# Large on-chip tiles moved to multiples of 512 bytes in a two-layer hybrid backbone

## The chip, the cores and the metric

The kernel runs on one core of a Trainium2 chip. The metric is the device time of one execution in microseconds (us), the median of several runs.

## What is computed

Two layers (DEPTH = 2) over 256 latent tokens and 256 context tokens of width 1024, all in float32. Each layer is a SwiGLU feed-forward block, a token mixer and a second SwiGLU block; each of the three takes its input through a shift and a scale, and its output goes through a gate, is added to the scaled residual and normalised. Shift, scale and gate come from a conditioning vector by a wide matrix, `w_ada`.

```
def ffn_sublayer(xs, m, j, wg, wu, wd, g, b):
    y = MACARON * swiglu(modulate(xs, m, j), wg, wu, wd)
    return residual_post_norm(xs, m[3 * j + 2] * y, g, b)
...
for l in range(DEPTH):
    m_lat = (jax.nn.silu(c) @ w_ada[l] + b_ada[l])...
    x_lat = ffn_sublayer(x_lat, m_lat, 0, ff1_gate[l], ff1_up[l], ff1_down[l], ...)
    x_ctx = ffn_sublayer(x_ctx, m_ctx, 0, ff1_gate[l], ff1_up[l], ff1_down[l], ...)
    y_lat, y_ctx = hybrid_mixer(modulate(x_lat, m_lat, 1), modulate(x_ctx, m_ctx, 1), ...)
    x_lat = residual_post_norm(x_lat, m_lat[5] * y_lat, ...)
    x_lat = ffn_sublayer(x_lat, m_lat, 2, ff2_gate[l], ff2_up[l], ff2_down[l], ...)
```

The mixer has neighbourhood attention (8 heads), a bidirectional gated recurrence and a Fourier branch, between one input and one output projection. The feed-forward width is 2816.

## The kernel before, in words

Activations are held transposed: 128 partitions are 128 of the 1024 channels, `xT[:, j, :]` is channel block j of 8, and its 512 columns are the 256 context and the 256 latent tokens. The large products are made at near float32 accuracy from three float32r matmuls: activations are split into a rounded part and a remainder (`hH`, `hL` for the input of a block, `aH`, `aL` for its middle), weights into `whi` and `wlo`, and hi x hi, hi x lo and lo x hi are summed (`mmh`, line 391). Each matmul has weights of 128x128 and streams 256 columns. Their results are named `gu` (gate and up), `dn` (down), `head` and `pj` (input projection of the mixer) and `wo` (output projection). `sc` are the attention scores, made from the tiles `k` and `q`.

Weights come in pieces of 128x1024 float32 (512 KB, `raw`, five buffers, issued on SP's queue at lines 254 and 256), ScalarE rounds a piece to `whi` (line 274), and VectorE, or for some pieces GpSimd, subtracts to get `wlo` (line 591). Rows of `w_ada` come through the same five buffers and are multiplied into `acc` and `fold` tiles by VectorE (lines 298 to 304). The first 15 us load x and the context into `in` tiles (line 237) and the constants into `cs`, and TensorE transposes x to `xT`.

The order of the whole program is fixed in the code (lists `seq` and `ORDER`). The on-chip memory is laid out by the order in which the pools are opened and, in the pool `const`, by the order in which the tiles are asked for; each tile begins at the next multiple of 32 bytes of a partition. A partition's row of a `raw`, `whi`, `wlo` or `acc` tile is 4096 bytes, of the tiles in the pool `scr` (tag "s", 13 buffers, with `k`, `sg`, `pr`, `h32` and others) 2048 bytes.

Of the kernel before, what the change touches and what calls it, by code (L numbers as in the profile page):

```python
# [11 lines left out]
F32 = mybir.dt.float32  # L12
# [7 lines left out]
DEPTH = 2  # L20
D = 1024
KD = D // 128
# [43 lines left out]
def kernel(ctx: ExitStack, tc: tile.TileContext, x, cx, vecs, cst, bias, w_ada,  # L66
# [3 lines left out]
    const = ctx.enter_context(tc.tile_pool(name="const", bufs=1))  # L70
# [10 lines left out]

    V, S, G, PE = nc.vector, nc.scalar, nc.gpsimd, nc.tensor

    xT = const.tile([128, KD, 512], F32, name="xT")
    hH = const.tile([128, KD, 512], F32R, name="hH")
    hL = const.tile([128, KD, 512], F32R, name="hL")
# [7 lines left out]
    SN = cs[:, 896:1408].rearrange("p (a b) -> p a b", a=2)  # L94
    vT = const.tile([128, V_ROWS], F32, name="vT")
    onesD = const.tile([128, 128], F32, name="onesD")
    one_c = const.tile([128, 1], F32, name="one_c")
    pick = const.tile([128, 2, 2], F32, name="pick")
    scol = const.tile([128, KD, 2], F32, name="scol")
    join = const.tile([128, 2], F32, name="join")  # L100
    bmean = const.tile([128, 6], F32, name="bmean")
    kcol = const.tile([128, 8], F32, name="kcol")
    lbd = const.tile([128, 8, 128], F32, name="lbd")
    fbd = const.tile([128, 2, 128], F32, name="fbd")
    AB = const.tile([128, 2, 2, 128], F32, name="AB")
    scol_z = AB[:, 0].rearrange("p a (k s) -> p (a k) s", s=32)
    mcol = [const.tile([128, 2, 72], F32, name=f"mcol{l}") for l in range(DEPTH)]

    def vcol(name, i, n=1):
        o = V_OFF[name] + i  # L110
# [1300 lines left out]
```

## Time and profile before

| | us |
|---|---|
| median of 3 runs (lowest, highest) | 1830.83 (1827.59, 1833.77) |
| the profiled execution | 1830.9 |
| its span, first to last instruction | 1829.0 |
| TensorE busy | 1751.4 |
| VectorE busy | 1224.8 |
| ScalarE busy | 700.6 |
| GpSimd busy | 327.9 |

The mean granted TensorE clock over the span is 0.983. Busy times overlap one another, so they do not add up to the span; 1.9 us of the execution lie outside it.

### The profile page before, as it was taken

The numbers are of one execution on the slowest core, as the hardware profiler recorded it, in microseconds if no ns is written. First come the engines' busy times: TensorE is split into PE (matmuls) and PEld (weight loads), VectorE is DVE, ScalarE is ACT, GpSimd is POOL, SyncE is SP. The second block draws the span as 40 slices with busy tenths as digits, with TensorE's granted clock in tenths as the row PEclk, the third lists the DMA queues.
The fourth block names the chain that finished last, engine by engine and source line by source line (L and its number), as shares of the span: only waits on it lengthen the run. The fifth ranks groups of instructions, "written<-read, shape, count | busy, mean of one in ns | idle before, by whom it ended". The sixth has DMA issues, their size and how long they took to land.

```text
span 1829.0 us, 33865 instructions
## 1 busy us (share of the span) xinstructions
PE 1751.4 (96%) x14241; PEld 1698.2 (93%) x14241; DVE 1224.8 (67%) x1867; ACT 700.6 (38%) x1119; POOL 327.9 (18%) x258
## 2 busy tenths in 40 slices
PE   7999999999899999999999999999999988979997
PEld 5999999998788999999999999999999868869997
DVE  3799899837586488755664569844643759666555
ACT  2232222225756564312222363222222565555443
POOL 0142122215441061000000140000000545140000
PEclk9999999999999999999999999999999999989998
DMA  7566555532223226544453226555653233266662
GB/s 263 181 195 187 170 167 170 171 95 81 69 59 93 59 82 180 162 139 136 132 157 114 86 81 196 166 171 166 178 169 88 81 93 93 82 192 192 177 190 80
DMA packets 375080, 253.33 MB, mean 139 GB/s; under 512 B 8144, under 2 KB 336336, under 8 KB 374928
## 3 DMA queue, kind: packets, MB, share of 16 engines
q1 hardware_dynamic: 373856, 248.81, 46.3%
q8 instruction: 112, 1.84, 0.4%
q0 software_dynamic: 1072, 2.36, 0.4%
q14 instruction: 40, 0.33, 0.1%
HBM read 250.09 MB, written 1.05 MB: 137 GB/s over the span
## 4 chain that ended last, share of the span: by engine, by line
PE 79%; DVE 15%; ACT 3%; issue 2%; DMA 0%; POOL 0%; SPq 0%; DVEq 0%; ACTq 0%
PE gu L391 42%; PE dn L391 21%; PE head L391 5%; PE pj L391 3%; PE wo L391 2%; DVE acc L304 2%; PE adat L332 1%; DVE ri L903 1%; DVE wlo L591 1%; PE o L1097 1%; DVE xl L870 1%; DVE s L460 1%; DVE xT L718 1%; DVE s L463 1%; PE adap L315 1%
## 5 line engine op out<-in xcount | busy, mean ns | idle before, releaser
L391 PE MATMUL gu<-hH,whi 128*128 128x256 f32 x2336 | 500.1, 283 | 2.0 <-ACT hH L1262 1.8
L391 PE MATMUL gu<-hH,wlo 128*128 128x256 f32 x2336 | 497.4, 282 | 2.1 <-DVE wlo L591 2.1
L391 PE MATMUL gu<-hL,whi 128*128 128x256 f32 x2336 | 497.6, 282 | 1.2 <-DVE hL L591 1.1
L274 ACT CAST whi<-raw 128x1024 fp32r<-128x1024 f32 (+1 forms) x319 | 318.8, 1024 | 284.3 <-PE dn L391 104.8
L591 POOL TENSOR_TENSOR wlo<-raw,whi 128x1024 fp32r<-128x1024 f32 (+2 forms) x106 | 207.7, 1966 | 1191.3 <-ACT whi L274 1153.7
L391 PEld LDWEIGHTS gu<-hH,whi 128*128 128x128 f32 x2336 | 374.1, 190 | 5.9 <-ACT hH L1262 2.6
L391 PEld LDWEIGHTS gu<-hH,wlo 128*128 128x128 f32 x2336 | 373.9, 190 | 2.6 <-DVE wlo L591 2.6
L391 PEld LDWEIGHTS gu<-hL,whi 128*128 128x128 f32 x2336 | 374.1, 190 | 1.7 <-DVE hL L591 1.7
L591 DVE TENSOR_TENSOR wlo<-raw,whi 128x1024 fp32r<-128x1024 f32 (+1 forms) x245 | 295.5, 1209 | 92.8 <-ACT whi L274 89.5
L391 PE MATMUL dn<-aH,whi 128*128 128x256 f32 x1280 | 286.3, 283 | 0.8 <-DVE xT L718 0.8
L391 PE MATMUL dn<-aH,wlo 128*128 128x256 f32 x1280 | 283.6, 281 | 0.0
L391 PE MATMUL dn<-aL,whi 128*128 128x256 f32 x1280 | 283.6, 281 | 0.0
L304 DVE SCALAR_TENSOR_TENSOR acc<-raw,scol,acc 128x512 f32<-128x512 f32 x337 | 275.2, 864 | 1.0
L731 ACT CAST aH<-pr 128x512 fp32r<-128x512 f32 (+1 forms) x88 | 50.0, 568 | 422.9 <-DVE pr L730 422.9
L391 PEld LDWEIGHTS dn<-aH,whi 128*128 128x128 f32 x1280 | 208.7, 189 | 1.4 <-DVE xT L718 1.2
L391 PEld LDWEIGHTS dn<-aH,wlo 128*128 128x128 f32 x1280 | 208.7, 189 | 0.1
L391 PEld LDWEIGHTS dn<-aL,whi 128*128 128x128 f32 x1280 | 208.7, 189 | 0.0
L730 DVE TENSOR_TENSOR pr<-sg,gu 128x512 f32<-128x512 f32 (+1 forms) x84 | 51.5, 614 | 148.7 <-PE gu L391 146.2
L718 DVE SCALAR_TENSOR_TENSOR xT<-dn,gate,xT 128x256 f32<-128x256 f32 x174 | 78.0, 478 | 90.5 <-PE dn L391 90.0
L729 ACT ACTIVATE sg<-gu 128x512 f32<-128x512 f32 (+1 forms) x84 | 45.3, 539 | 115.5 <-PE gu L391 115.3
L391 PE MATMUL pj<-hH,whi 128*128 128x256 f32 x384 | 84.5, 288 | 4.9 <-DVE k L591 2.7
L391 PE MATMUL pj<-hH,wlo 128*128 128x256 f32 x384 | 83.1, 285 | 0.0
(239 smaller groups left out, 2127.7 us busy)
## 6 DMA issues: line engine op xcount, KB each, us to landing
raw<-in_w_ada_dram SPq DMA_DIRECT2D x136, 512.0 KB, 4.6
raw<-in_ff_gate_dram SPq DMA_DIRECT2D x88, 512.0 KB, 4.4
raw<-in_ff_up_dram SPq DMA_DIRECT2D x88, 512.0 KB, 4.8
raw<-in_ff_down_dram SPq DMA_DIRECT2D x64, 448.0 KB, 4.5
raw<-in_w_in_dram SPq DMA_DIRECT2D x36, 512.0 KB, 3.9
raw<-in_ff_down_dram SPq DMA_DIRECT2D x32, 512.0 KB, 4.8
raw<-in_w_out_dram SPq DMA_DIRECT2D x16, 512.0 KB, 4.1
in<-in_w_ada_dram SPq DMA_DIRECT2D x8, 512.0 KB, 6.9
```

Of the source, the lines that this page charges most:

```text
L274: S.copy(h_[:, :n], t[:, :n])
L304: V.scalar_tensor_tensor(out=a[:, st], in0=t[:, kk * 512:(kk + 1) * 512], scalar=sc_, in1=a[:, st], op0=ALU.mult, op1=ALU.add)
L315: PE.matmul(acc[l, b][32 * (k % 4):32 * (k % 4) + 32, :], lhsT=scol_z[:, k, :], rhs=t[:, kk * 512:(kk + 1) * 512], start=(k < 4), stop=(k ...
L332: PE.matmul(tp[:, q * 2:q * 2 + 2], lhsT=a[:, q * 128:(q + 1) * 128], rhs=w, start=True, stop=True)
L391: PE.matmul(o[:, c], lhsT=w, rhs=X[:, k, c], start=first and i == 0, stop=last and i == len(halves) - 1)
L460: (e1 or V).tensor_tensor(out=s1, in0=a, in1=z, op=ALU.add)
L463: (e2 or V).tensor_tensor(out=s2, in0=b, in1=sq, op=ALU.add)
L591: (eng or V).tensor_tensor(out=dst_l, in0=src, in1=dst_h.bitcast(F32), op=ALU.subtract)
L718: V.scalar_tensor_tensor(out=xT[:, j, a:b], in0=ps[:, a:b], scalar=gate[:, st, j:j + 1], in1=xT[:, j, a:b], op0=ALU.mult, op1=ALU.add)
L729: S.activation(out=sg[:, c], in_=gp[:, c], func=AF.Silu)
L730: V.tensor_tensor(out=pr[:, c], in0=sg[:, c], in1=up[:, c], op=ALU.mult)
L731: S.copy(aH[:, m, c], pr[:, c])
```

## The change

The six small constants and the two tables of modulation columns (`mcol`, 576 bytes each) are asked for first, then a pad tile of 32 bytes that nothing uses, then the large tiles in their old order.

```
+    one_c = const.tile([128, 1], F32, name="one_c")
+    pick = const.tile([128, 2, 2], F32, name="pick")
+    scol = const.tile([128, KD, 2], F32, name="scol")
+    join = const.tile([128, 2], F32, name="join")
+    bmean = const.tile([128, 6], F32, name="bmean")
+    kcol = const.tile([128, 8], F32, name="kcol")
+    mcol = [const.tile([128, 2, 72], F32, name=f"mcol{l}") for l in range(DEPTH)]
+    const.tile([128, 8], F32, name="pad")
     xT = const.tile([128, KD, 512], F32, name="xT")
     hH = const.tile([128, KD, 512], F32R, name="hH")
...
     onesD = const.tile([128, 128], F32, name="onesD")
-    one_c = const.tile([128, 1], F32, name="one_c")
-    pick = const.tile([128, 2, 2], F32, name="pick")
-    scol = const.tile([128, KD, 2], F32, name="scol")
-    join = const.tile([128, 2], F32, name="join")
-    bmean = const.tile([128, 6], F32, name="bmean")
-    kcol = const.tile([128, 8], F32, name="kcol")
     lbd = const.tile([128, 8, 128], F32, name="lbd")
...
-    mcol = [const.tile([128, 2, 72], F32, name=f"mcol{l}") for l in range(DEPTH)]
```

The start of each tile in its partition, in bytes, and what is left of it modulo 512:

| tiles | before | left | after | left |
|---|---|---|---|---|
| xT (then hH, hL, aH, aL) | 16512 | 128 | 17920 | 0 |
| cs, vT, onesD | 98432 and on | 128 | 99840 and on | 0 |
| lbd, fbd, AB | 106336 and on | 352 | 107520 and on | 0 |
| raw, whi, wlo (5 buffers each) | 114656 and on | 480 | 114688 and on | 0 |
| in, acc, fold, zt, q (6 buffers) | 176096 and on | 480 | 176128 and on | 0 |
| scr: k, sg, pr, h32 and others (13 buffers) | 200672 and on | 480 | 200704 and on | 0 |
| one_c, pick, scol, join, bmean, kcol | 106112 and on | 128 to 320 | 16512 and on | 128 to 320 |
| mcol0, mcol1 | 113504, 114080 | 352, 416 | 16736, 17312 | 352, 416 |

The instructions, their shapes, their waits and their order are the same on all five engines, and so are the DMAs and their order on each queue. Addresses in the chip's main memory do not change.

## Rows read from the trace of the kernel before

**Rows 1.** The page's head and engines: busy us (share of span), instructions.

```profile
span 1829.0 us, 33865 instructions
...
PE 1751.4 (96%) x14241; PEld 1698.2 (93%) x14241; DVE 1224.8 (67%) x1867; ACT 700.6 (38%) x1119; POOL 327.9 (18%) x258
```

**Rows 2.** The page's chain that ended last, by engine.

```profile
PE 79%; DVE 15%; ACT 3%; issue 2%; DMA 0%; POOL 0%; SPq 0%; DVEq 0%; ACTq 0%
```

**Rows 3.** Windows: busy us (count) PE, PEld, DVE, ACT, POOL; granted clock, DMA share, GB/s.

```profile
100.00:400.00 300.00, 298.63 (x2520) 298.05 (x2519) 252.63 (x372) 74.78 (x91) 68.53 (x33) 0.99 0.57 166
...
1000.00:1030.00 30.00, 30.00 (x256) 30.00 (x255) 13.87 (x20) 9.35 (x12) 0.00 (x0) 1.00 0.29 84
...
1680.00:1710.00 30.00, 30.00 (x258) 30.00 (x257) 15.91 (x21) 11.79 (x15) 0.00 (x0) 1.00 0.66 188
```

**Rows 4.** The chain in order of time: start us, us, what.

```profile
820.06 56.43 PE gu L391 x480
```

**Rows 5.** Groups by form: busy us, mean ns of one, idle before.

```profile
L391 PE MATMUL gu<-hH,whi 128*128 128x256 f32 x2336 | 500.1, 283 | 2.0 <-ACT hH L1262 1.8
...
L391 PE MATMUL dn<-aH,wlo 128*128 128x256 f32 x1280 | 283.6, 281 | 0.0
...
L391 PE MATMUL pj<-hH,wlo 128*128 128x256 f32 x384 | 83.1, 285 | 0.0
...
L391 PE MATMUL head<-hH,wlo 128*128 128x256 f32 x256 | 65.5, 288 | 0.0
...
L391 PE MATMUL wo<-aH,wlo 128*128 128x256 f32 x144 | 33.9, 281 | 0.0
```

**Rows 6.** Timeline of TensorE: start us, us until the last ends, instructions.

```profile
525.41 0.40 PE L391 MATMUL pj<-hL,whi 128*128 128x256 f32 x2
...
526.35 0.40 PE L1005 MATMUL sc<-k,q 128*128 128x512 f32 x1
...
527.28 0.40 PE L391 MATMUL pj<-hH,whi 128*128 128x256 f32 x2
...
527.75 0.41 PE L391 MATMUL pj<-hL,whi 128*128 128x256 f32 x2
```

**Rows 7.** Timeline of TensorE, and the window around it, at the lower clock.

```profile
39.88 0.63 PE L391 MATMUL gu<-hH,whi 128*128 128x256 f32 x2
40.31 0.63 PE L391 MATMUL gu<-hL,whi 128*128 128x256 f32 x2
...
38.90:41.10 2.20, 2.20 (x12) 2.20 (x12) 0.00 (x0) 0.00 (x0) 0.00 (x0) 0.50 0.72 262
```

**Rows 8.** Two tiles' instructions on VectorE: ns min/median/max, first and last start.

```profile
L591 DVE TENSOR_TENSOR aL<-pr,aH x88: 417/684/694, 84.0 to 1796.0; 128x512 fp32r<-128x512 f32 x66, 128x256 fp32r<-128x256 f32 x22
...
L356 DVE TENSOR_TENSOR fold<-fold x24: 677/684/693, 104.5 to 1189.5; 128x512 f32<-128x512 f32 x24
```

**Rows 9.** Windows, columns as in rows 3.

```profile
0.00:15.00 15.00, 7.47 (x34) 6.21 (x35) 3.69 (x15) 2.96 (x5) 1.82 (x8) 1.00 0.87 314
...
1650.00:1680.00 30.00, 30.00 (x259) 30.00 (x258) 19.06 (x26) 17.46 (x28) 0.00 (x0) 1.00 0.69 197
```

**Rows 10.** Waits of TensorE: us in total, times, longest us.

```profile
PE vtp L1236 <- DMA cs<-in_cst_dram: 4.6, 1, 4.6
...
PE gu L391 <- DVE wlo L591: 2.1, 2, 1.6
...
PE xtp L1271 <- DMA in<-in_x_dram: 1.6, 2, 0.8
...
PE xtp L1271 <- DMA in<-in_ctx_dram: 0.7, 1, 0.7
```

**Rows 11.** The chain in order of time, at the start.

```profile
3.17 7.05 DMA in<-in_x_dram
```

**Rows 12.** Waits of ScalarE for weights, columns as in rows 10.

```profile
ACT whi L274 <- DMA raw<-in_ff_down_dram: 63.2, 15, 9.1
```

**Rows 13.** DMA issues: count, KB each, median us to landing.

```profile
raw<-in_ff_gate_dram SPq DMA_DIRECT2D x88, 512.0 KB, 4.4
```

## The prediction

> **What bounds the kernel now.** I read the busy shares first. TensorE is busy for 1751.4 of 1829.0 us, VectorE for two thirds of it [rows 1]. A busy TensorE need not be a limiting one, so I read the chain of work that ended last next: 79% of it is TensorE, 15% VectorE, 3% ScalarE, and DMA rounds to 0% [rows 2]. Third, the stretches by window: far from the edges TensorE is busy 30.00 of 30 us and issues 256 to 258 matmuls in them, whether the DMA engines are 29% or 66% busy [rows 3]. So TensorE issues one matmul every 117 or 118 ns and waits for nobody. In the chain this reads 56.43 us for 480 matmuls of `gu`, 117.6 ns each [rows 4].
>
> Nearly all of them have one form, weights of 128x128 against 256 moving columns in float32r. The groups show 2336 for each of three operand pairs in `gu`, 1280 in `dn`, 384 in `pj`, 256 in `head`, 144 in `wo` [rows 5]: 3 x 4400 = 13200. At 117.6 ns that is 1552 us, 85% of the span. The rest is the mixer with its short matmuls, the norms, and 15 us at the start.
>
> **The change, part by part.** It moves addresses only. The sequence on every engine and queue is the same, and the pad tile has no instruction. So nothing can come from a step that is earlier or later; time can come only from instructions or DMA packets that run at another speed because their tiles begin elsewhere. Before, no large tile begins at a multiple of 512 bytes: xT, hH, hL, aH, aL, the constants, vT and onesD stand 128 past one, lbd, fbd and AB 352 past, all pools of large tiles 480 past. The trace therefore has rows of large tiles at 128, 352 and 480, and none at 0. I ask for each engine whether 128 and 480 differ, and whether its price has room for a misaligned start.
>
> *TensorE.* `pj` matmuls stream hH or hL (remainder 128) against weights at 480. `sc` matmuls stream k and load q, both at 480. They stand next to each other [rows 6]: eight `pj` of 256 columns take 525.41 to 526.35, 117.5 ns each; four `sc` of 512 columns (one of the four stands there) take 526.35 to 527.28, 232.5 ns each, 116 per 256 columns; the next four `pj` take 0.47 us, 117.5 again. So the remainder of the moving tile makes no difference that these rows can show. [...] I take 0 for TensorE. [...]
>
> *VectorE and ScalarE.* aL <- pr, aH reads from 480 and 128 and writes to 128; fold <- fold reads and writes at 480. Both are tensor-tensor operations on 512 columns, both take 684 ns at the median [rows 8], and their longest differ by 1 ns. I take 0. Bound: 1 ns either way on each of the 1867 VectorE and 1119 ScalarE instructions [rows 1] is 3 us in all, of which the chain, with 18% of its length on these two engines [rows 2], would see some 0.5 us.
>
> *DMA.* Every weight transfer lands at 480, in runs of 512 bytes (2 KB for w_ada). A stretch with weights only moves 197 GB/s at a share of 0.69, so 286 GB/s if the engines were always busy; the first 15 us, with runs of 2 to 5 KB beside them, 314 at 0.87, so 361 [rows 9]. One engine has a sixteenth of that: 512 bytes take 28.6 ns in the one and 22.7 in the other. The 5.9 ns between them are what a run costs beside its bytes, and the most that a better start could give back: a fifth of the DMA time. The least is nothing, and no row shows a loss.
>
> [...]
>
> What is it worth? TensorE waits for a DMA in three places, all in the first 11 us, 6.9 us in all: for the constants, x and the context [rows 10]. The chain has one DMA piece, 7.05 us until x has landed [rows 11]. The four transfers of x and context have 4 KB runs, 128 each, so 8 per engine and transfer: 32 x 5.9 ns = 0.2 us if all of the surcharge goes, 1.5 us if the whole piece became a fifth shorter. Later ScalarE does wait for weights, 63.2 us for the down weights alone [rows 12], but TensorE does not wait behind it: its waits for wlo before `gu` are 2.1 us in all [rows 10]. Those are the cover of the DMA, and they bound what faster landing can add: 1.5 + 2.1 = 3.6 us at most. I take 0.2, because the wait is for 4 KB runs, whose surcharge I can count.
>
> **Sum.** The profiled execution took 1830.9 us, its span of 1829.0 and 1.9 around it; the median of three runs is 1830.83, so it stands for them. 1830.9 - 0 (TensorE) - 0 (VectorE, ScalarE) - 0.2 (DMA) = 1830.7 us.
>
> **Rivals.**
> [...]
> 2. *The DMA gain reaches further.* The whole piece at the start and all waits for wlo shrink: 3.6 us, so 1827. That stays inside 0.3% of the time, 5.5 us, which is about what a measurement of this kernel can tell from none. To pass it, the gain would have to free ScalarE's casts at places where TensorE waits for something else, such as the heads of the mixer. Chance 10%, a third of it past 0.3%.
> 3. *Slower: equal starts collide.* Before, the stream (128) and the weights (480) of the main matmuls begin 352 bytes apart, modulo 512; afterwards both begin at 0. If reading both at one offset costs TensorE a little, it costs it 13200 times: 0.42 ns each is 5.5 us and decides; the 2.5 ns that the rows leave would be 33 us, 1864. Against it: `sc` already has both at 480, and its columns are no dearer than those of `pj` [rows 6]; fold has all operands at one offset, and takes what aL takes [rows 8]. Chance 6%.
> 4. *The layout is not what the words say.* Excluded: the built program has xT at 35 x 512 bytes and each large tile behind it at a multiple; only the small per-norm tiles stay at multiples of 32.
>
> **How the numbers follow.** My forecast, no change beyond 0.3%, has 80%, rival 1 4%, rival 2 10%, rival 3 6%. The three runs of before spread from 1827.59 to 1833.77, 0.17% either side, so two medians can differ by a little over 0.3% with no cause; I give 3% to each side for that, out of the 80. Faster: 4 + 3 + 3 = 10%, slower: 6 + 3 = 9%, same: 81%. The range: from the forecast, the bounds of DMA (-3.6) and of VectorE and ScalarE (0.5) and the spread of the runs (3 either way) reach 1823 to 1835; a part of rival 3, up to 0.3 ns per matmul, adds 4 above. 1823 to 1839 leaves out rival 1, the far end of rival 2 and most of rival 3, under 2 in 10.
>
> **What would show it.** [...] VectorE: 684 ns for aL and fold. DMA: 286 GB/s for a full share from 1650 to 1680 means that the landing address does not matter; 350 or more that it does, and then the landing time of 4.4 us [rows 13] falls by some 0.4 us and the chain still shows DMA at 0%. What would make me wrong is a price that no row before can show, since no large tile stood at remainder 0.

## The result, and the profile after

The changed kernel is slower. Its median is 1850.37 us (1848.84 to 1851.91, four runs), that of the kernel before 1831.72 (1827.59 to 1833.77, four runs); the ratio is 1.0105, with a 95% interval from 1.0084 to 1.0125. I had forecast 1830.7 within 1823 to 1839, and given 6% to the rival that happened.

The profiled execution took 1850.85 us, its span 1849.1. The page's head and engines, columns as in [rows 1], with the line of the weights' queue:

```profile
span 1849.1 us, 33865 instructions
...
PE 1775.8 (96%) x14241; PEld 1723.3 (93%) x14241; DVE 1224.4 (66%) x1867; ACT 700.4 (38%) x1119; POOL 329.1 (18%) x258
...
q1 hardware_dynamic: 373856, 248.81, 44.9%
```

TensorE is busy for 24.4 us more, the other engines for what they were. Its idle time (span less busy) went from 77.6 to 73.3 us: 24.4 more work less 4.3 of waiting is the span's 20.1. Then windows of the changed kernel, to set beside [rows 3] and [rows 9]:

```profile
1000.00:1030.00 30.00, 30.00 (x253) 30.00 (x252) 9.95 (x14) 7.71 (x10) 0.00 (x0) 1.00 0.27 81
...
1650.00:1680.00 30.00, 30.00 (x253) 30.00 (x253) 15.46 (x22) 19.10 (x31) 1.13 (x3) 1.00 0.64 194
1680.00:1710.00 30.00, 30.00 (x253) 30.00 (x252) 18.03 (x25) 13.88 (x17) 0.00 (x0) 1.00 0.72 208
```

TensorE issues 253 matmuls in 30 us, not 256 to 259, at the same granted clock of 1.00 (a window also counts the two or three that reach over its edges). The chain's long piece of `gu` answers to [rows 4]; it was 56.43 us:

```profile
826.39 57.70 PE gu L393 x480
```

That is 120.2 ns for a matmul in place of 117.6, slower as rival 3 has it. VectorE's rows have not moved, as the tiles of [rows 8] show:

```profile
L593 DVE TENSOR_TENSOR aL<-pr,aH x88: 417/684/694, 83.5 to 1815.8; 128x512 fp32r<-128x512 f32 x66, 128x256 fp32r<-128x256 f32 x22
...
L358 DVE TENSOR_TENSOR fold<-fold x24: 676/684/691, 103.9 to 1200.6; 128x512 f32<-128x512 f32 x24
```

And the start: TensorE's three waits for DMAs [rows 10] are in sum 0.7 us shorter, and the chain's one DMA piece [rows 11] is 0.5 us shorter.

```profile
PE vtp L1238 <- DMA cs<-in_cst_dram: 3.5, 1, 3.5
...
PE xtp L1273 <- DMA in<-in_x_dram: 1.6, 2, 0.8
PE xtp L1273 <- DMA in<-in_ctx_dram: 1.1, 2, 0.8
```

```profile
3.17 6.58 DMA in<-in_x_dram
```

So the loss is in the price of one matmul: 24.4 us over 13200 are some 1.85 ns on each. The question is what in the addresses sets that price.

### The profile page after: what moved, and what is told of

The parts are those of the page before. It is cut to its first block, busy times and chain, and to the rows that moved or that the text cites. A ratio compares the mean times of both kernels' runs of the same rounds, so it can differ in the third digit from the quotient of the medians.

```text
span 1849.1 us, 33865 instructions
## 1 busy us (share of the span) xinstructions
PE 1775.8 (96%) x14241; PEld 1723.3 (93%) x14241; DVE 1224.4 (66%) x1867; ACT 700.4 (38%) x1119; POOL 329.1 (18%) x258
## 3 DMA queue, kind: packets, MB, share of 16 engines
q1 hardware_dynamic: 373856, 248.81, 44.9%
## 4 chain that ended last, share of the span: by engine, by line
PE 79%; DVE 14%; ACT 4%; issue 3%; DMA 0%; POOL 0%; SPq 0%; DVEq 0%; ACTq 0%
PE gu L393 41%; PE dn L393 21%; PE head L393 5%; PE pj L393 3%; PE wo L393 2%; DVE acc L306 2%; PE adat L334 1%; DVE ri L905 1%; DVE wlo L593 1%; PE o L1099 1%; DVE xl L872 1%; DVE xT L720 1%; DVE s L462 1%; DVE s L465 1%; PE adap L317 1%
## 5 line engine op out<-in xcount | busy, mean ns | idle before, releaser
L393 PEld LDWEIGHTS gu<-hH,whi 128*128 128x128 f32 x2336 | 379.6, 193 | 5.9 <-ACT hH L1264 2.5
L393 PEld LDWEIGHTS gu<-hH,wlo 128*128 128x128 f32 x2336 | 379.6, 193 | 2.5 <-DVE wlo L593 2.5
L393 PEld LDWEIGHTS gu<-hL,whi 128*128 128x128 f32 x2336 | 379.8, 193 | 1.7 <-DVE hL L593 1.7
L720 DVE SCALAR_TENSOR_TENSOR xT<-dn,gate,xT 128x256 f32<-128x256 f32 x174 | 78.1, 479 | 95.3 <-PE dn L393 94.7
```

Source lines behind the costliest of these rows:

```text
L393: PE.matmul(o[:, c], lhsT=w, rhs=X[:, k, c], start=first and i == 0, stop=last and i == len(halves) - 1)
L720: V.scalar_tensor_tensor(out=xT[:, j, a:b], in0=ps[:, a:b], scalar=gate[:, st, j:j + 1], in1=xT[:, j, a:b], op0=ALU.mult, op1=ALU.add)
```

## The experiments

Three theories: the price hangs on where the weights begin; on where the streamed tile begins; or on the distance between the two starts. "Distance" is the start of the weights less that of the streamed tile, modulo 256 bytes: 96 before (480 - 128 = 352), 0 after. In all versions that compute the result the instructions and their order are those of the kernel before; only addresses differ.

**One half of the change at a time.** `pools_only` has the pad behind the old list of constants, `const_only` has the changed order, opens the small pools sm and dv ahead of the weights and pads again:

```
     mcol = [const.tile([128, 2, 72], F32, name=f"mcol{l}") for l in range(DEPTH)]
+    const.tile([128, 8], F32, name="pad")
```

> A pad behind the constants alone: weights and the other pools begin at 0, xT, hH, hL, aH, aL stay at 128. If the price hangs on where the weights begin, every main matmul takes 120.0 ns as after the change, and the time is 1850 us. If it hangs on where the streamed tile begins, 118.1 ns and 1831 us. If it hangs on the distance between the two modulo 512 (352 bytes before, 0 after), it is 128 less 0, a distance not seen yet: some price from 115 to 122 ns, 1831 us if only equal starts are dear.

```
+    sm = ctx.enter_context(tc.tile_pool(name="sm", bufs=6))
+    dv = ctx.enter_context(tc.tile_pool(name="dv", bufs=2))
     wraw = ctx.enter_context(tc.tile_pool(name="wraw", bufs=5))
...
     AB = const.tile([128, 2, 2, 128], F32, name="AB")
+    const.tile([128, 24], F32, name="padb")
```

> The other half: xT, hH, hL, aH, aL and the constants begin at 0, weights and the other large pools at 480. By the theory of the weights' start 118.1 ns and 1831 us, by that of the streamed tile's start 120.0 ns and 1850 us, by that of the distance (480 bytes now) 1831 us if only equal starts are dear.

`pools_only` took 1837.04 us, ratio 1.0031 (1.0020 to 1.0042); `const_only` 1819.39, ratio 0.9939 (0.9920 to 0.9958). The weights' move alone costs 6 us, that of the streamed tiles gains 12, and both together cost 19. Two effects that each hang on one start would add up; these do not, so both single-start theories fall.

**A map of prices.** A kernel of matmuls alone, 48 in each block, in which the block's name says the streamed tile's and the weights' place modulo 512 (this map and the two below ran once each):

```
for a in range(0, 128, 8):        # streamed tile, in elements of 4 bytes
    for b in range(0, 128, 8):    # weights
        block(a, b)   # 8 k x ((WH, XH), (WL, XH), (WH, XL)) x 2 halves of 256 columns
```

> Leaves out all of the computation: 256 blocks of 48 matmuls of the kernel's main form (weights 128x128, 256 moving columns, float32r, the kernel's order of hi and lo), each block with the streamed tile and the weights at another multiple of 32 bytes modulo 512, 16 x 16 of them. The theory of the weights' start expects 16 equal rows (a block's time depends on the weights' offset alone), that of the stream's start 16 equal columns, that of the distance equal diagonals, with 120 ns (5.76 us a block) where both are 0 and 118 ns (5.67 us) at stream 128, weights 480. No dependence on alignment at all: 256 equal blocks, and the 1% of the change comes from something outside TensorE's reads.

The chain of `map_fine` in order of time, the blocks with the streamed tile at 64, and two with it at 96 and 128:

```profile
208.91 5.75 PE m064w064x L87 x48
214.66 5.68 PE m064w096x L87 x48
220.33 5.66 PE m064w128x L87 x48
225.99 5.63 PE m064w160x L87 x48
231.62 5.69 PE m064w192x L87 x48
237.31 5.75 PE m064w224x L87 x48
243.06 5.65 PE m064w256x L87 x48
248.71 5.66 PE m064w288x L87 x48
254.37 5.75 PE m064w320x L87 x48
```

```profile
317.02 5.47 PE m096w160x L87 x48
...
464.72 5.63 PE m128w480x L87 x48
```

The price goes round once in 256 bytes: distance 0 takes 5.75 us, 96 takes 5.63, 160 again 5.75, and 256 is 0 again. The blocks at other streams repeat it shifted by as much, but for the few named below: equal diagonals, neither rows nor columns. From the starts of the matmuls in a block (all but the first eight) the typical means are, for distances 0, 32, 64, 96, 128, 160, 192, 224: 120.0, 118.4, 117.8, 117.4, 118.7, 119.9, 117.8 and 117.8 ns. This kernel gives no other engine an instruction between the first block and the last, so the price moves from 117.4 to 120.0 ns without any other engine's work. At distance 0 every matmul takes 120 ns exactly, after some seven; elsewhere the price mostly swings from one matmul to the next, at 96 from 115 to 120. Twelve blocks fell into another pattern than the rest of their diagonal: four of the 32 at distance 64, `m096w160x` one of them, take 113.3 ns; the four at distance 96 that run straight after these take 120.0; and four at distance 224 take 116.7. So the distance alone does not settle the price. Whether it is the place of the stream or the block that ran before is not shown. (The map's first block, whose first matmuls took 213 ns, is left out of the means.)

```profile
322.49 5.76 PE m096w192x L87 x48
```

**Distances in the program itself.** Small constants go to a pool opened last, or a pad follows them, so that the weights begin at other places; the streams stay at 128. `same128` moves three of them, `d032` two, `d064` one; `d160` pads by 64 bytes and `d192` by 96:

```
     dv = ctx.enter_context(tc.tile_pool(name="dv", bufs=2))
+    late = ctx.enter_context(tc.tile_pool(name="late", bufs=1))
...
-    one_c = const.tile([128, 1], F32, name="one_c")
+    one_c = late.tile([128, 1], F32, name="one_c")
```

> No large tile at a multiple of 512: the streamed tiles stay at 128, three small tiles (one_c, pick, join) go to a pool opened last, so weights and the other pools begin at 384, distance 256. If the distance of the two starts modulo 256 sets the price, as the map's diagonals say, this is the change's distance of 0: 120.0 ns for a main matmul, without jitter, and 1850 us. If a start at a multiple of 512 were what costs, it is as before: 1831 us.

> One small tile (one_c) goes to a pool opened last; weights begin at 448, distance 64 from the stream modulo 256. By the map 117.8 ns in 28 of 32 blocks, 113.3 in the other four: worked from the changed kernel (120.0 ns, 1850 us) and 13200 matmuls, 1821 us, and 1762 if the program falls into the shorter pattern throughout. If only equal starts cost, 1831.

> A pad of 64 bytes behind the constants: streams at 128, weights at 32, distance 160 modulo 256. By the map 119.9 ns: 1849 us, as dear as equal starts, though the two are far apart. If only equal starts cost, 1831.

> Two small tiles (one_c, pick) go to a pool opened last; weights at 416, distance 32 modulo 256. By the map 118.4 ns: 1829 us. If nearness of the two starts costs, it lies close to the changed kernel, 1845 to 1850.

> A pad of 96 bytes behind the constants: streams at 128, weights at 64, distance 192 modulo 256. By the map 117.8 ns: 1821 us, as const_only and d064. If some other thing than the distance made those two faster than before, it need not appear here.

In the table, "program" is the price read from the version's own trace: the mean from start to start of its 13200 main matmuls, at the granted clock of 1.00 and without the intervals over 135 ns, which hold a wait (some 12,900 are left). The ratio is to runs of before made together with the version's; the time of before is the range of its medians.

| version | distance | map, ns | program, ns | time, us | ratio to before (95%) |
|---|---|---|---|---|---|
| after | 0 | 120.0 | 119.9 | 1850.37 | 1.0105 (1.0084 to 1.0125) |
| same128 | 0 | 120.0 | 119.9 | 1852.92 | 1.0122 (1.0104 to 1.0140) |
| d160 | 160 | 119.9 | 120.0 | 1850.30 | 1.0110 (1.0088 to 1.0132) |
| pools_only | 128 | 118.7 | 118.7 | 1837.04 | 1.0031 (1.0020 to 1.0042) |
| d032 | 32 | 118.4 | 118.3 | 1831.28 | 1.0011 (0.9999 to 1.0023) |
| before | 96 | 117.4 | 118.1 | 1829.6 to 1831.7 | 1 |
| d192 | 192 | 117.8 | 117.7 | 1826.18 | 0.9984 (0.9974 to 0.9993) |
| d064 | 64 | 117.8 | 117.1 | 1823.25 | 0.9963 (0.9950 to 0.9976) |
| const_only | 224 | 117.8 | 116.9 | 1819.39 | 0.9939 (0.9920 to 0.9958) |

`same128` is the decisive one: no large tile starts at a multiple of 512, and the loss of the change is there in full. `d160` is as slow with starts far apart, so nearness is not it either. The chain of these two and of `d064`, the same piece of `gu`:

```profile
827.91 57.70 PE gu L392 x480
```

```profile
824.29 57.71 PE gu L392 x480
```

```profile
816.35 56.64 PE gu L392 x480
```

The expectations from the map hold within 3 us for four of the five versions made to test it; `d192` is 5 us off. The version before is out of line: 96 is the cheapest distance of the map, and only fourth here. Its own chain shows why. Beside the 117.6 ns of [rows 4] it has pieces at 119:

```profile
964.20 45.68 PE gu L391 x384
1080.74 45.57 PE gu L391 x384
```

One distance can hold more than one pattern, and the mean over all of its main matmuls is 118.1. The same goes for `d064`, where about one stretch of 24 matmuls in nine runs at 113.5 ns, and for `const_only`, where most stretches run at 116.7, the price of the four odd blocks at its distance. By the price in the program, and not by that of the map, the versions stand in the order of their times, the three at 120 ns together at the top; before and `d032`, 0.2 ns apart, are not told apart by their times.

**Which side of the read.** Blocks with other lengths of stream (n) and of weights (m), at eight distances (d); the loops here and below are shown without the blocks' names:

```
for n in (512, 256, 128):         # streamed columns
    for m in (128, 64, 32):       # columns of weights
        for b in range(0, 64, 8): # distance, in elements
            block(b, n, m)
```

> Leaves out all of the computation: 72 blocks of 48 float32r matmuls with 512, 256 or 128 streamed columns, 128, 64 or 32 columns of weights, and 8 distances from 0 to 224 bytes. [...]

The chain of `map_parts`, some of the 72 blocks:

```profile
61.17 10.91 PE n512m128d000x L86 x48
72.08 11.19 PE n512m128d032x L86 x48
...
327.98 5.75 PE n256m128d000x L86 x48
...
345.06 5.63 PE n256m128d096x L86 x48
...
418.32 5.65 PE n256m032d000x L86 x48
...
429.62 5.46 PE n256m032d064x L86 x48
...
484.06 5.36 PE n128m128d128x L86 x48
```

The blocks were to tell two theories apart: if the price comes from the load of the next weights, it falls with their columns, and so does its spread over the distances; if it belongs to the stream alone, it is the same for 128 and 32 columns of weights. Neither held. With 256 streamed columns and 32 of weights the price is still 113.3 to 117.8 ns, where 128 have 117.4 to 120.0: a quarter of the weights' columns takes only some 2 to 4 ns off, and the price still hangs on the distance. With 64 columns of weights it goes from 113.3 to 119.1 ns, and distance 0 is the cheapest. With 128 streamed columns and 128 of weights the distance does nothing (5.31 to 5.36 us in all eight blocks, 112 ns). And with 512 streamed columns and 128 of weights distance 0 is the cheapest of the eight (227 ns), where with 256 it is the dearest. So which distance is good depends on the form of the matmul.

**Mixtures.** The kernel's three products read whi or wlo against hi or lo streams. With hH at 0, each of hL (l), whi (h) and wlo (w) at 8 places:

```
for xl in range(0, 64, 8):
    for wh in range(0, 64, 8):
        for wl in range(0, 64, 8):
            block(xl, wh, wl)
```

> Leaves out all of the computation: 512 blocks of 48 main matmuls in the kernel's order, with hH at 0 and each of hL, whi and wlo at 8 places from 0 to 224 bytes modulo 256. If each matmul's price followed its own distance alone, a block would cost the mean of its three kinds: 117.4 to 120.0 ns, no less than the best single distance. If the pattern over several matmuls matters (the jitter repeats over some five of them, and one distance had blocks of 113.3), some mixtures lie outside these ends, below 117 ns or above 120.

```profile
61.12 5.76 PE l000h000w000x L87 x48
...
186.19 5.45 PE l000h064w192x L87 x48
...
345.15 5.49 PE l000h192w064x L87 x48
```

Two of 512 mixtures stand at 113.3 ns, with whi at 64 and wlo at 192 or the reverse, though each place alone has 117.8; the dearest has 121.5. Half of all blocks lie between 117.8 and 118.8. So a matmul's price is not its own distance's; the sequence makes it. I put both mixtures into the program, by pools between and behind the weights:

```
+    mid = ctx.enter_context(tc.tile_pool(name="mid", bufs=1))
     wlo_p = ctx.enter_context(tc.tile_pool(name="wlo", bufs=5))
...
+    one_c = mid.tile(...)   # and pick, join, bmean: 128 bytes between whi and wlo
+    kcol = late.tile(...)
```

(`hi064lo192` puts scol and the second mcol into the last pool too.)

> The six constants are spread over two small pools so that whi begins 192 bytes and wlo 64 bytes behind the streamed tiles modulo 256; nothing else. The map of hi and lo has this mixture at 113.3 ns without jitter and its neighbours at 115.5 to 116.5: 1850 us less 13200 times 6.7 ns is 1762 us, 1797 at 116 ns. If each matmul's price followed its own distance alone, 117.8 ns as in d064 and d192: 1823 to 1826 us.

> The same with whi and wlo exchanged: whi 64 and wlo 192 bytes behind the streams. In the map its block also stands at 113.3 ns, but its neighbours cost 117 to 120: 1762 us if the program falls into that pattern and stays in it, some 1830 if it is thrown out of it at the pauses of TensorE. By each matmul's own distance 1823 to 1826 us.

`hi192lo064` took 1790.15 us, ratio 0.9767 (0.9743 to 0.9791), `hi064lo192` 1784.73, ratio 0.9749 (0.9733 to 0.9765): 45 us less than before and the best of all versions. The prices in the program are 114.4 and 113.6 ns. Their chains, the first of `hi192lo064`, the second of `hi064lo192`:

```profile
803.17 54.58 PE gu L393 x480
...
1655.82 39.95 PE gu L393 x336
```

```profile
802.72 54.53 PE gu L393 x480
...
1653.81 38.08 PE gu L393 x336
```

With both halves of the tokens (first lines) both versions run at 113.6 to 113.7 ns. In the last block, where only the latent half is left and each piece of weights meets one stream and not two, `hi192lo064` is thrown back to 118.9 while `hi064lo192` keeps 113.3; I had expected the second to be the fragile one, and why it is the first is not shown. Why the gain is 66 us from the changed kernel and not the 88 of the forecast shows in `hi064lo192`'s page:

```profile
span 1782.6 us, 33865 instructions
...
PE 1697.7 (95%) x14241; PEld 1643.9 (92%) x14241; DVE 1224.9 (69%) x1867; ACT 700.6 (39%) x1119; POOL 328.2 (18%) x258
```

TensorE is busy for 78.1 us less than after the change, of which 11.6 come back as idle time (84.9 us against 73.3): where the next input comes from another engine, a shorter matmul only lengthens the wait. Two such waits, first after the change, then in `hi064lo192`:

```profile
PE m L470 <- DVE s L462: 4.5, 5, 1.1
...
PE adat L334 <- DVE fold L358: 0.5, 1, 0.5
```

```profile
PE m L470 <- DVE s L462: 6.1, 5, 1.5
...
PE adat L334 <- DVE fold L358: 3.6, 3, 2.6
```

The other 10 us were never saved. Some 4 of them are the way into the pattern: a stretch of matmuls often takes some ten to reach 113.3 ns, so that the price fell by 6.4 ns in the mean (119.9 to 113.6) and not by 6.7. Another 3 to 5 are the lower clock (granted 0.50), at which a main matmul takes 213 ns in both versions: some 190 ran there in `hi064lo192`, some 160 after the change.

## Why the prediction was wrong

*What bounds the kernel* was right: TensorE issues back to back, so most of a price on its main matmul reaches the end time (24.4 us of work, 20.1 of span).

*The change moves addresses only, and time can come only from instructions that run at another speed*: right. VectorE and ScalarE at 0: right, 684 ns in both of VectorE's rows, and ScalarE is busy for 700.4 us against 700.6.

*DMA at -0.2 us, at most -1.5*: inside its bounds, but not shown as a gain of the change. The piece at the start is 0.5 us shorter (6.58 us), and as short in `d160` (6.57), where no large tile starts at a multiple of 512. Nor does the weights' queue show a gain that hangs on the landing address: its packets took 46.3% of 1829.0 us before (847 us) and 44.9% of 1849.1 after (830), 2% less and not the fifth that I had put as the most, and a full share moves 289 to 303 GB/s against 285, not 350. The 2% are not due to the start either: in `same128` the weights land at 384 modulo 512, and the queue took 44.7% of 1850.4 us, 827. The queue before and in `same128`, and the piece in `d160`:

```profile
q1 hardware_dynamic: 373856, 248.81, 46.3%
```

```profile
q1 hardware_dynamic: 373856, 248.81, 44.7%
```

```profile
3.18 6.57 DMA in<-in_x_dram
```

*TensorE at 0*: this is the step that failed. I took 0 because `pj` and `sc` matmuls cost the same per column [rows 6], and used the same rows against rival 3, as "sc already has both at 480, and its columns are no dearer". Three things were wrong with that. The `sc` matmuls there have 512 columns, and `map_parts` shows that for 512 distance 0 is the cheapest of all (227 ns), for 256 the dearest (120). They are four in a row, while the map's blocks need some seven to fall into the 120 ns pattern: the trace of before also has `sc` of 256 columns, with both tiles at 480, and four of them take the 0.47 us between the two starts below, 117.5 ns each and not 120. And the view behind [rows 4] holds the pieces at 119 ns shown above, beside the one of 117.6 that I read: the price of one form was not one number even in one layout.

```profile
562.16 0.28 PE L1005 MATMUL sc<-k,q 128*128 128x256 f32 x1
...
562.63 0.40 PE L391 MATMUL pj<-hH,whi 128*128 128x256 f32 x2
```

The rows, written to 10 ns, could over four matmuls only bound the price to 2.5 ns either way; the truth, 1.85 ns, lay inside that bound, and 13200 times it was outside my range. The weight of 6% rested on the argument and not on the bound.

*Rival 3* named the place, the count and the sign. That both at one offset are dear is half of it: distance 0 takes 120.0 ns in the map, but 160 takes 119.9, and the price is one of a pattern over several matmuls. That the two reads collide no run shows.

*Rival 1* (a faster TensorE) fell for this change, whose long piece of `gu` went from 117.6 to 120.2 ns a matmul. But the price that I took for fixed does move with the addresses, in the maps from 120.0 ns at distance 0 to 113.3 in two mixtures; no block with 256 streamed columns came under 113.3.

What stays open is what makes the pattern. The runs show on what it depends (the distance of the starts modulo 256 bytes, the lengths, how hi and lo follow each other, how many matmuls run in a row); none shows the mechanism.

## What to carry to other kernels

Where TensorE issues back to back, an address is a parameter worth a few per cent (1784.7 to 1852.9 us here): measure the price of the main matmul over the distance of its two operands modulo 256 bytes, in one kernel of bare matmuls in the program's own order, before choosing a layout. Then read the price again in the program: it lay up to 0.7 ns above the map's (before) and 0.9 ns below it (`const_only`). Round addresses are not better ones; here the round layout was among the worst. And a difference too small to see in one row counts when it is taken thirteen thousand times: where a bound times a count is larger than the range, the range must hold it.

## What the runs showed of the hardware that was not expected

- A float32r matmul of 256 columns, at the same granted clock of 1.00, takes from 113.3 to 121.5 ns in the maps, by where its operands and its neighbours' begin, with no other engine at work.
- Sequences of such matmuls settle: into 120 ns exactly at distance 0, into 113.3 in the two mixtures, into swings such as 115 to 120 at 96, and one distance can hold several patterns (at 96 also 120 exactly in the map).
- Where the granted clock is 0.50, a main matmul takes 213 ns at the median before, after and in `hi064lo192`: there the address makes no difference that these rows show.
- With the distance alone changed, and no instruction for any other engine, the typical price of a matmul in `map_fine` changed by 2.6 ns (117.4 at distance 96, 120.0 at 0), along equal diagonals: neither the stream's start nor the weights' sets it alone.
- Transfers in runs of 512 bytes took the same DMA time within 3% at three starts: 847 us at 480 modulo 512, 830 at 0, 827 at 384.
